# Attention on one core: the first batch's last K chunk and three Q tiles are staged in the next batch's V room

## Chip, cores, metric

The kernel runs on 1 core of one Trainium2 chip. The metric is device time in microseconds (us) of one execution; a profile also gives the span, some 2 us shorter. A run is taken as fast unless it is over 1.5% above the fastest of the same kernel. "PE" is the matrix engine, "DVE" the vector engine, "ACT" the scalar engine, "POOL" the engine that issues all converting loads, "SP" the one that issues stores and DMA transposes.

## The reference

Eight independent batches of softmax attention, sequence 2048, width 512, 32-bit:

```python
scores = np.matmul(q, k.transpose(0, 2, 1)) / np.sqrt(d_k)
attn_weights = special.softmax(scores, axis=-1)
return np.matmul(attn_weights, v)          # q, k, v: (8, 2048, 512)
```

## The kernel before

K, Q and V come in loads of 128 x 4 x 512 (1 MB read as 32-bit, 512 KB written as 16-bit), four to a batch and tensor. K and Q go to one of four staging buffers and are transposed from there, in the first batch by PE (except Q tiles 2 and 3), later by DMA. V goes straight to its own room, of which there are two, one for each of two neighbouring batches. The matmuls are in a Strassen-like form (seven products of half blocks in place of eight), so DVE makes sums of K, Q, V and P blocks beside them ("background"). A group `g` is one Q tile of 512 rows: four to a batch, 32 in all.

```python
stage = ctx.enter_context(tc.tile_pool(name="stage", bufs=4))
vpool = ctx.enter_context(tc.tile_pool(name="vpool", bufs=2))
# ... cut
def load(what, b, c, pieces=(CH,)):
    t = staged.get((what, b, c))
    if t is None:
        t = staged[what, b, c] = stage.tile([P, CH, D], F16, tag="stage", name="stage")
    n = CH - sum(pieces)
    for w in pieces:
        at = c * CH + n
        nc.gpsimd.dma_start(out=t[:, n:n + w, :], in_=srcs[what][b, :, at:at + w, :])
        n += w
# ... cut
def new_v(b):                       # V room: two memsets on POOL set its column of ones
    vh = vpool.tile([P, NJ, 2, VP], F16, tag="vh")
    t1 = vpool.tile([P, NJ, TP], F16, tag="t1")
    # ... cut
    nc.gpsimd.memset(vh[:, :, 1, D:D + 1], 1.0)
    nc.gpsimd.memset(t1[:, :, H:H + 1], 1.0)
# ... cut: what is fetched when, as (tile of the batch, slot)
    (0, 0, "newv"), (0, 2, "load", "v", 0), (0, 8, "load", "v", 1), # ... cut
    (1, 16, "load", "k", 0), (1, 26, "trans", "k", 0), (2, 8, "sum", "k", 0),
    (2, 8, "load", "k", 2), # ... cut
# ... cut: batch 1's loads are held back by a copy that needs P of group 1
            if what[0] == "newv":
                if g == 1:
                    nc.gpsimd.tensor_copy(out=gate[:], in_=pts[g][0][0][:, NJ - 1, 0:1])
                new_v(bb)
# ... cut: the start. k0 and q0 come through SP, in blocks
gate = const.tile([P, 1], F32)
nc.gpsimd.tensor_copy(out=gate[:], in_=firsts["q", 1][:, 0:1])
load("k", 0, 1, (2, 2))
load("k", 0, 2)
new_v(0)
load_v(0, 0)
# ... cut: transposes of k0, q0, k1 and the first score blocks on PE
load("k", 0, 3)
load("q", 0, 1)
for c in range(1, NCH):
    load_v(0, c)
for kb in range(2 * G, NKB):
    plain_tile(0, kb)
    # ... cut: PE transposes of k1, k2, k3, q1; DVE sums
load("q", 0, 2)
load("q", 0, 3)
```

The softmax here doesn't subtract the row's maximum and nothing guards it: scores larger than these inputs give would overflow.

## Time and profile before

| | before |
|---|---|
| time, median of 3 runs | 808.3 us (807.66 to 808.34) |
| span of the profiled run | 807.0 us |
| PE busy | 797.8 us, 99% |
| PE's waits in the first 60 us / after | 5.4 us / none |
| PE's wait for K chunk 3 | 1.36 us, from 20.93 to 22.29 |
| first product with V | 33.60 us |

PE sets the time; everything else matters only where it makes PE wait. The lines behind this table stand in the prediction below. In the profile's lines `stage` is a staging buffer, `vh` the V room, `raw` a transposed K or Q tile, `ks` and `qs` the sums made of such tiles, `cz` a piece of the scores that DVE adds up, `tr` and `t` PE's output banks.

### The profile page before, as it was taken

The page shows a single profiled execution, that of the slowest core. Times are in us where ns is not written, and L with a number is a line of the kernel's source. Part 1 is how long each engine was busy: PE and PEld are TensorE (multiplying, and loading weights), DVE is VectorE, ACT ScalarE, POOL GpSimd, SP SyncE. Part 2 cuts the span into 40 slices and gives each one's busy share as a digit, 9 for nine tenths or more (in the row PEclk, how much of TensorE's full clock was granted, in tenths as well). Part 3 has the DMA queues.
Part 4 walks back from the last instruction along what each step waited for, and adds up shares of the span by engine and source line. Part 5 has one row for each costly group of instructions (what it writes and reads, how often), then busy time and mean ns, then how long its engine had stood idle before and what let it go on. Part 6 is the DMA issues. An engine that isn't in the chain of part 4 may idle for free.

```text
span 807.0 us, 18446 instructions
## 1 busy us (share of the span) xinstructions
PE 797.8 (99%) x7244; PEld 704.6 (87%) x7244; DVE 591.0 (73%) x1477; ACT 570.2 (71%) x1039; POOL 72.5 (9%) x117
## 2 busy tenths in 40 slices
PE   8999999999999999999999999999999999999998
PEld 4688888888888888888888888888888888888887
DVE  4877787787767778677777777777777777766653
ACT  5767767677677677677677677777777776776773
POOL 4020103000030000300003000020002001000000
PEclk9999999999999999999999999999999999999999
DMA  9949995989379893898929997299972999921112
GB/s 206 198 91 190 211 166 106 205 161 171 92 130 213 154 168 82 145 208 153 164 79 148 219 151 149 69 177 191 162 164 62 190 200 154 155 71 48 54 40 79
DMA packets 190246, 116.56 MB, mean 144 GB/s; under 512 B 124496, under 2 KB 172880, under 8 KB 190160
## 3 DMA queue, kind: packets, MB, share of 16 engines
q0 software_dynamic: 49648, 49.29, 39.9%
q1 hardware_dynamic: 140368, 66.08, 39.5%
q8 instruction: 56, 0.92, 0.5%
q14 instruction: 30, 0.25, 0.1%
q10 hardware_dynamic: 144, 0.03, 0.0%
HBM read 100.70 MB, written 33.55 MB: 166 GB/s over the span
## 4 chain that ended last, share of the span: by engine, by line
PE 93%; DMA 4%; DVE 2%; ACT 0%; issue 0%; SPq 0%; DVEq 0%; ACTq 0%
PE t L378 47%; PE t L295 45%; DMA out_dram<-o 2%; DMA stage<-in_k_dram 1%; DMA cz<-in_q_dram 1%; PE t L233 0%; DVE cz L321 0%; PE tr L143 0%; DVE o L389 0%; SPq L115 0%; DVE raw L146 0%; DVE s L338 0%; DVE t L213 0%; DVE right L340 0%; DVE vh L211 0%
## 5 line engine op out<-in xcount | busy, mean ns | idle before, releaser
L295 PEld LDWEIGHTS <-raw 128*128 128x128 f16 x1984 | 194.1, 98 | 23.4 <-issue 0.6
L386 ACT ACTIVATE o<-t,r 128x256 f32<-128x256 f32 x256 | 122.2, 477 | 129.5 <-DVE r L406 104.0
L295 PE MATMUL t<-raw 128*128 128x256 f16 x1488 | 203.0, 273 | 0.0
L223 ACT ACTIVATE left<-t 128x512 f16<-128x512 f32 (+1 forms) x264 | 156.4, 594 | 21.8 <-PE t L295 19.3
L378 PEld LDWEIGHTS <-s 128*128 128x128 f16 x1536 | 150.3, 98 | 18.7 <-issue 0.4
L295 PEld LDWEIGHTS <-ks 128*128 128x128 f16 x1488 | 145.6, 98 | 18.2 <-issue 1.2
L389 DVE SCALAR_TENSOR_TENSOR o<-t,r,o 128x256 f32<-128x256 f32 x192 | 92.3, 481 | 81.2 <-PE t L378 48.6
L295 PE MATMUL t<-qs,ks 128*128 128x256 f16 x992 | 139.0, 273 | 0.5 <-ACT t L308 0.4
L223 ACT ACTIVATE right<-cz 128x1024 f16<-128x1024 f32 x124 | 132.5, 1068 | 1.5 <-DVE cz L318 1.5
L378 PE MATMUL t<-t,s 128*128 128x257 f16 (+1 forms) x1024 | 133.0, 273 | 0.0
L378 PE MATMUL t<-vh,left 128*128 128x256 f16 x1024 | 132.7, 273 | 0.0
L312 ACT COPY cz<-t 128x512 f32<-128x512 f32 x124 | 72.7, 586 | 67.3 <-PE t L295 67.3
L378 PEld LDWEIGHTS <-right 128*128 128x128 f16 x1024 | 100.2, 98 | 12.2 <-issue 0.6
L318 DVE TENSOR_TENSOR cz<-t,cz 128x512 f32<-128x512 f32 x124 | 85.1, 686 | 34.6 <-PE t L295 34.6
L378 PEld LDWEIGHTS <-left 128*128 128x128 f16 x1024 | 100.2, 98 | 11.6
L321 DVE TENSOR_TENSOR cz<-t,cz 128x512 f32<-128x512 f32 x124 | 84.7, 683 | 2.1 <-PE t L295 2.1
L295 PE MATMUL t<-qs,raw 128*128 128x256 f16 x496 | 74.4, 273 | 0.5 <-DVE cz L318 0.5
L295 PE MATMUL t<-raw,ks 128*128 128x256 f16 x496 | 74.4, 273 | 0.0
L338 DVE TENSOR_TENSOR s<-right 128x512 f16<-128x512 f16 x128 | 53.9, 421 | 27.5 <-ACT right L223 22.8
L315 ACT COPY cz<-t 128x512 f32<-128x512 f32 x124 | 73.1, 590 | 0.2 <-PE t L295 0.2
L308 ACT COPY t<-t 128x512 f32<-128x512 f32 x124 | 70.7, 570 | 3.3 <-ACT o L386 0.3
L378 PE MATMUL t<-vh,s 128*128 128x257 f16 x512 | 66.7, 273 | 0.1
(47 smaller groups left out, 611.6 us busy)
## 6 DMA issues: line engine op xcount, KB each, us to landing
out_dram<-o SPq DMA_DIRECT2D x127, 256.0 KB, 2.9
vh<-in_v_dram POOLq DMA_DIRECT2D x32, 512.0 KB, 13.8
stage<-in_q_dram POOLq DMA_DIRECT2D x31, 512.0 KB, 12.5
stage<-in_k_dram POOLq DMA_DIRECT2D x30, 512.0 KB, 8.5
raw<-stage SPq DMA_TRANSPOSE x58, 6.8
first<-in_q_dram SPq DMA_DIRECT2D x2, 256.0 KB, 3.7
first<-in_k_dram SPq DMA_DIRECT2D x2, 256.0 KB, 4.1
cz<-in_q_dram SPq DMA_DIRECT2D x2, 256.0 KB, 5.4
```

Of the source, the lines that this page charges most:

```text
L223: nc.scalar.activation(out=out_, in_=in_, func=EXP, scale=inv_sqrt_d)
L295: nc.tensor.matmul(dst[:, j * QH:(j + 1) * QH], lhs[:, j, c, :], rhs[:, :, c, :], start=(n in (1, 5) and j == 0 and c == 0), stop=(c == 1) ...
L308: nc.scalar.copy(out=self.y[:], in_=self.x[:])
L312: nc.scalar.copy(out=self.cz[:, :, 1, :], in_=self.two(self.z))
L315: nc.scalar.copy(out=self.cz[:, :, 0, :], in_=self.two(self.x))
L318: nc.vector.tensor_add(self.cz[:, :, 1, :], self.two(self.x), self.cz[:, :, 1, :])
L321: nc.vector.tensor_add(self.cz[:, :, 0, :], self.two(self.z), self.cz[:, :, 0, :])
L338: lambda: add(s1[:, js], a21, a22),
L378: nc.tensor.matmul(dst[:, 0:width], lhs(j), rhs(j), start=(first and j == 0), stop=(j == NJ - 1), skip_group_check=True,)
L386: nc.scalar.activation(out=out_, in_=src, func=COPY, scale=r[:])
L389: nc.vector.scalar_tensor_tensor(out=out_, in0=src, scalar=r[:], in1=out_, op0=MULT, op1=ADD)
```

## The change

The intent: in the first batch, four of the loads wait for a staging buffer to come free, and PE waits for one of them, K chunk 3. Batch 1's V room is empty then. K chunk 3 and Q tiles 1 to 3 are staged there, so that POOL issues all loads in one row, K chunk 3 and Q tile 1 ahead of V.

```diff
-    def load(what, b, c, pieces=(CH,)):
+    def load(what, b, c, pieces=(CH,), room=None):
         t = staged.get((what, b, c))
+        if room is not None:
+            t = staged[what, b, c] = room
         if t is None:
@@
+    spare = vpool.tile([P, NJ, 2, VP], F16, tag="vh", name="vh")
+    spare = spare[:].rearrange("p j s d -> p (j s d)")[:, 0:4 * CH * D]
+    spare = spare.rearrange("p (t n d) -> p t n d", t=4, n=CH)
     load("k", 0, 1, (2, 2))
     load("k", 0, 2)
+    load("k", 0, 3, room=spare[:, 0])
+    load("q", 0, 1, room=spare[:, 1])
     new_v(0)
-    load_v(0, 0)
+    for c in range(NCH):
+        load_v(0, c)
+    load("q", 0, 2, room=spare[:, 2])
+    load("q", 0, 3, room=spare[:, 3])
@@
-    load("k", 0, 3)
-    load("q", 0, 1)
-    for c in range(1, NCH):
-        load_v(0, c)
@@
-    load("q", 0, 2)
-    load("q", 0, 3)
```

## The prediction

> **What bounds the kernel now.** I read the page's busy shares first, then what the matrix engine waits for, then its instructions in order of time around the waits, then the POOL row of load issues with their landing times.
>
> ```profile
> PE 797.8 (99%) x7244; PEld 704.6 (87%) x7244; DVE 591.0 (73%) x1477; ACT 570.2 (71%) x1039; POOL 72.5 (9%) x117
> PE 93%; DMA 4%; DVE 2%; ACT 0%; issue 0%; SPq 0%; DVEq 0%; ACTq 0%
> ```
>
> The first line is busy time of each engine, the second the chain that ended last. The kernel is a stream of matmuls: 797.8 of the 807.0 us of span. Whatever touches only transfers can earn no more than PE's idle time, 807.0 - 797.8 = 9.2 us, less the 3.4 us after PE's last matmul (802.56 + 1.04 = 803.60). All of PE's waits, with the releaser (total us, times, longest):
>
> ```profile
> PE tr L143 <- DMA stage<-in_k_dram: 1.4, 1, 1.4
> PE t L537 <- DVE warm L510: 1.2, 1, 1.2
> PE tr L143 <- DVE stage L119: 0.9, 1, 0.9
> PE tr L143 <- ACT stage L119: 0.7, 1, 0.7
> PE t L295 <- DVE cz L318: 0.5, 1, 0.5
> PE t L295 <- ACT t L308: 0.4, 1, 0.4
> PE tr L143 <- DVE raw L146: 0.3, 1, 0.3
> ```
>
> That is 5.4 us, all in the first 60 us; the same view from 60 us on is empty. One line, the first, is a wait for one of the loads that the change moves. The others lie at the very start (warm, first tiles rounded to 16 bit) or are waits for DVE and ACT. PE in order of time, start and us, with the idle time before it in brackets:
>
> ```profile
> 17.31 3.62 PE L233 MATMUL t<-raw 128*128 128x512 f16 x16
> 22.29 1.07 PE L143 MATMUL tr<-ident,stage 128*128 128x128 f16 x16 [1.35 <-DMA stage<-in_k_dram]
> 23.19 2.75 PE L233 MATMUL t<-raw 128*128 128x512 f16 x12
> ```
>
> PE stops at 17.31 + 3.62 = 20.93 and starts the transposes of K chunk 3 (the program's last K chunk) at 22.29. The gap is 1.36 us, and the load it waits for is read from POOL's row:
>
> ```profile
> 6.60 2.29 POOL L105 DMA_DIRECT2D stage<-in_k_dram  x3
> 8.95 0.77 POOL L202 DMA_DIRECT2D vh<-in_v_dram  x1
> 10.22 0.75 POOL L105 DMA_DIRECT2D stage<-in_k_dram  x1 [0.51 <-DVE raw L146]
> 12.35 0.74 POOL L105 DMA_DIRECT2D stage<-in_q_dram  x1 [1.38 <-ACT right L223]
> 13.08 2.23 POOL L202 DMA_DIRECT2D vh<-in_v_dram  x3
> 15.95 0.74 POOL L105 DMA_DIRECT2D stage<-in_q_dram  x1 [0.64 <-PE tr L143]
> 17.77 0.74 POOL L105 DMA_DIRECT2D stage<-in_q_dram  x1 [1.08 <-PE tr L143]
> ```
>
> The third line is K chunk 3: issued 10.22 and, by the chain of waits, 12.02 us to landing, so there at 22.24. The brackets are waits for a staging buffer to come free, the waits that the change removes. Landing times (issue plus time to landing, each issue taken alone in the list of DMA issues; v2 and v3 from medians of two): k2 8.13+8.2 = 16.3; v0 8.95+10.9 = 19.85; k3 22.24; q1 12.35+12.5 = 24.85; v1 13.08+14.3 = 27.4; v2 29.9; v3 32.5; q2 15.95+19.0 = 34.95; q3 17.77+20.2 = 38.0. From k3 to q2 they land one every 2.55 us (12.7 us for five), whatever the spacing of their issues (0.74 to 2.1 us). The queue is therefore limited by transfer, not by issue: what counts is a load's place in the row, not its issue time.
>
> **What the Trainium skill says.** "DMA: Bandwidth & Descriptors", section Bandwidth, measures 425 GB/s for a large load and puts the ceiling at 435. A load here reads 1 MB of 32-bit data (128 x 4 x 512 x 4 B = 1.05 MB; the profile counts the 512 KB written), so 2.55 us each is 411 GB/s: the trace agrees that the row runs near its limit. The same page, section Queues, rings and completion order, says that each DMA engine takes descriptors in ring order; the landings in issue order agree. "SBUF — State Buffer", section SBUF: two separate sides, warns that certain DVE copies lock POOL out of writing descriptors; here POOL issues take 0.72 to 0.81 us with DVE copies beside them, so I give that little weight.
>
> **The change, part by part.** No engine but POOL changes its order: the compiled PE, DVE, ACT and SP streams hold the same operations in the same order, only the semaphore that a few wait on differs. POOL issues the same loads in the order k1 (two halves), k2, k3, q1, v0, v1, v2, v3, q2, q3.
>
> Removed: four buffer waits on POOL, 0.51 + 1.38 + 0.64 + 1.08 = 3.6 us of an engine that is 9% busy; not on the path. The row is not quite free: loads share eight completion semaphores, so v3 still waits for the first half of k1 to land (11.4), q2 for the second half (13.3), q3 for k2 (16.3). All three are early against a queue that is full to 35 us.
>
> Moved: k3 and q1 advance one place each, v0 falls back two. Giving each place its old landing time: k3 19.85 instead of 22.24, q1 22.24 instead of 24.85, v0 24.85 instead of 19.85; v1 to q3 keep theirs, because the bytes ahead of them are the same. (k3 could also gain a little because the row has no holes; I count none.)
>
> On the path: PE reaches k3's transposes at 20.93, and k3 is there at 19.85 with 1.08 us to spare. The 1.36 us gap goes. q1's transposes would start at 25.78 - 1.36 = 24.42, with q1 there since 22.24. Next, from 26.43 to 33.1, DVE is the bound (its chain starts at the copy that follows q1's transposes: "26.43 0.69 DVE raw L146"), and again from 41.9 to 49.0. Both start from PE's transposes, so they move as a block; DVE's order is fixed, so the gain neither grows nor shrinks there. From 60 us PE has no wait, and batch 1's loads hang on a gate on POOL that follows ACT (53.13), so they move along with the rest. Sum: 808.3 - 1.36 = 806.9 us.
>
> **Rivals.**
> 1. The wait moves to V. The first product with V starts at 33.60 and its fourth pair of matmuls, which needs v3, at about 33.60 + 6 x 0.109 = 34.25; moved up, 32.9, against v3's landing at 32.5. Only 0.4 us to spare: v3 landing a microsecond late gives back 0.6, time 807.5. For it: v3's place is unchanged while its user advances. Against: same bytes ahead.
> 2. k3 does not land on v0's old time. From 11 to 14 us the queue moved only 113 to 145 GB/s (as counted), against 206 later, and I do not know why; if more waiting loads lengthen that stretch, k3 lands after 20.93 and every microsecond beyond is lost. At k3 = 21.5 the time is 807.5; at 22.2, 808.2.
> 3. The gain is swallowed. q2's and q3's DMA transposes keep their absolute times (35.02 + 4.9 = 39.9; 38.1 + 4.8 = 42.9), but DVE first uses q2 at 47.15 - 1.36 = 45.8, 6 us later. Batch 1's V, whose room now holds k3 and the Q tiles, must wait for those transposes at 42.9, but its gate opens near 51.8. Neither bites: no loss.
> 4. More than the gap is won. DVE idles 2.50 us before k3's copy (22.94), which suggests up to 2.5; but 1.15 of it is PE's own transpose and copy latency, which stays. Time 805.8 only if it all counted.
>
> **Range and chances.** Full gain about 65%, partial (rivals 1 and 2) 25%, none or slightly worse 10%. Three runs of before spread over 0.7 us, so the median of after may stray half a microsecond by itself. Range 805.9 to 808.2. A change of over 2% is 16 us, and PE's whole waiting is 5.4, so faster by 2% is as good as excluded; slower by 2% would need a wait repeated in every batch, and later batches keep their order and waits.
>
> **What would show it.** Right: PE's list of waits without the K line and 1.4 us shorter in sum; PE busy through 21 to 22 us; k3 landing near 19.9, q1 near 22.2, v0 near 24.9, v3 still near 32.5; POOL's eleven loads without buffer waits, the last issued just after 16.3; DVE's block starting at 25.1 and the first product with V at 32.2. Wrong: a wait of PE for a V load near 33, k3 landing after 20.9, or a new wait after 60 us.

## The result, and the profile after

| | before | after |
|---|---|---|
| time, median of 4 runs | 808.32 us | 808.55 us (807.29 to 809.25) |
| ratio | | 0.9999, 95% interval 0.9982 to 1.0017 |
| span of the profiled run | 807.0 us | 807.4 us |
| first product with V | 33.60 us | 32.66 us |
| PE's waits after 60 us | none | 1.4 us |

A ratio is the mean time of one kernel's fast runs over that of the other's fast runs of the same rounds, so it is not quite the ratio of the medians quoted. The time did not change. All waits of PE in the changed kernel, with the releaser (us in total, times, longest; lines are numbered 2 to 11 higher than before):

```profile
PE t L548 <- DVE warm L512: 1.2, 1, 1.2
PE t L297 <- DVE cz L320: 0.9, 3, 0.5
PE t L297 <- DVE cz L323: 0.9, 1, 0.9
PE tr L145 <- DMA stage<-in_k_dram: 0.7, 2, 0.4
PE t L297 <- ACT t L310: 0.4, 1, 0.4
PE tr L145 <- DVE raw L148: 0.3, 1, 0.3
```

The list sums to 4.4 us, 1.0 less than before, but sums of waits do not compare the two starts: the 0.9 + 0.7 us for the first tiles (`stage L119`) are missing here, and PE ran its matmuls near 5 us slower instead (0.63 us for four transposes, not 0.39; the trace's first record of a fully granted clock is at 7.1 us, not 4.6). The 1.4 us for K chunk 3 are gone (the 0.7 us of `stage<-in_k_dram` are waits for the earlier chunks 1 and 2), but there is a new line, `cz L323`. First the part that was meant, PE in order of time (start, us, then the idle time before in brackets):

```profile
12.95 0.62 PE L145 MATMUL tr<-ident,stage 128*128 128x128 f16 x8 [0.41 <-DMA stage<-in_k_dram]
...
17.00 1.07 PE L145 MATMUL tr<-ident,stage 128*128 128x128 f16 x16 [0.30 <-DMA stage<-in_k_dram]
17.90 3.62 PE L235 MATMUL t<-raw 128*128 128x512 f16 x16
21.36 1.06 PE L145 MATMUL tr<-ident,vh 128*128 128x128 f16 x16
```

The transposes of K chunk 3 (they now read `vh`) start with no gap. POOL's row, in order of time:

```profile
6.62 2.43 POOL L107 DMA_DIRECT2D stage<-in_k_dram  x3
9.04 0.75 POOL L107 DMA_DIRECT2D vh<-in_k_dram  x1
...
13.18 0.74 POOL L204 DMA_DIRECT2D vh<-in_v_dram  x1 [0.34 <-DMA stage<-in_k_dram]
...
17.23 0.74 POOL L107 DMA_DIRECT2D vh<-in_q_dram  x1 [2.04 <-DMA stage<-in_k_dram]
```

No buffer waits are left, only those on the eight completion semaphores. K chunk 3 landed at 19.47, Q tile 1 at 21.98, V 0 at 24.52, V 3 at 32.16. At the first product with V PE is 0.94 us ahead of the kernel before, and stays so to 87 us. Then, near 91, PE in order of time:

```profile
91.59 1.03 PE L297 MATMUL t<-qs,ks 128*128 128x256 f16 x8 [0.89 <-DVE cz L323]
...
93.71 0.60 PE L297 MATMUL t<-qs,raw 128*128 128x256 f16 x4 [0.21 <-DVE cz L320]
```

The chain of waits leads back from there to one transfer (start, us, what):

```profile
73.41 15.50 DMA raw<-stage
...
88.92 0.44 DVE ks L175
...
90.86 0.68 DVE cz L323
```

It is the DMA transpose of batch 1's K chunk 0. DVE stands 3.2 us at the sum of that chunk (`ks L175`), and the additions PE needs (`cz`) come behind it on the same engine. The sum in DVE's order of time, before and after:

```profile
86.59 0.41 DVE L173 TENSOR_TENSOR ks<-raw 128x512 f16<-128x512 f16 x1
88.92 0.42 DVE L175 TENSOR_TENSOR ks<-raw 128x512 f16<-128x512 f16 x1 [3.18 <-DMA raw<-stage]
```

In the kernel before the same transpose was issued at 74.34 and took 10.2 us; it was there at 84.5, two us ahead of its sum at 86.59. In the changed kernel it took 15.5. The Trainium skill, "TensorE: Matmul & The Clock Gate", section Architectural detail, says that DVE's queue is strictly first in, first out; the trace agrees, as the `cz` additions did not pass the waiting sum. Both traces have all 7244 matmuls, so matmuls can be compared by their number: between the 700th and the 900th the changed kernel falls back by 1.42 us against the kernel before. This is where the gain went.

Why is that transpose late? Batch 1's row of loads is held back by the gate. POOL at that point, before:

```profile
53.13 0.18 POOL L486 CAST gate<-left 128x1 f32<-128x1 f16 x1 [34.62 <-ACT left L223]
53.25 0.13 POOL L195 MEMSET vh<- 128x8 f16 x1
...
53.73 0.75 POOL L105 DMA_DIRECT2D stage<-in_q_dram  x1 [0.30 <-PE t L295]
```

and after:

```profile
52.20 0.18 POOL L488 CAST gate<-left 128x1 f32<-128x1 f16 x1 [34.23 <-ACT left L225]
52.49 0.13 POOL L197 MEMSET vh<- 128x8 f16 x1
...
52.97 0.75 POOL L107 DMA_DIRECT2D stage<-in_q_dram  x1 [0.30 <-issue]
```

From gate to memset it is 0.12 us before and 0.29 after: the memset writes to the room in which K and Q were staged, and in the compiled order it now carries waits on seven semaphores instead of two, all long reached (the last transpose out of the room had landed at 42.26). The packed trace has the wait instructions: one ahead of the memset before (53.19), three after (52.21, 52.29, 52.38), 0.09 us apart; two more of them make the 0.17 us. It is not the other room: e_v_swap below trades the rooms and has 0.12 us. So the row starts 0.77 us after the gate instead of 0.60. SP's third output store does not move with it: it is issued 0.50 us after the row's first load before, 0.33 us after. In the trace's packets, the row's first one now comes 2.15 us after its issue instead of 1.46, behind the store's instead of ahead of them, and the row runs slower: its first load takes 8.0 us instead of 6.4, its seventh 26.4 instead of 23.1. What follows in this document tests that chain.

### The profile page after: what moved, and what is told of

It reads as the page before. It is cut to its first block, busy times and chain, and to the rows that moved or that the text cites. A ratio compares the mean times of both kernels' runs of the same rounds, so it can differ in the third digit from the quotient of the medians.

```text
span 807.4 us, 18443 instructions
## 1 busy us (share of the span) xinstructions
PE 799.1 (99%) x7244; PEld 705.4 (87%) x7244; DVE 590.3 (73%) x1477; ACT 570.4 (71%) x1039; POOL 72.8 (9%) x117
## 4 chain that ended last, share of the span: by engine, by line
PE 90%; DMA 6%; DVE 3%; issue 0%; ACT 0%; POOL 0%; SPq 0%; DVEq 0%; ACTq 0%
PE t L380 46%; PE t L297 44%; DMA raw<-stage 4%; DMA stage<-in_k_dram 1%; PE t L235 1%; DMA first<-in_q_dram 1%; PE tr L145 0%; DVE o L391 0%; DVE cz L323 0%; DVE cz L320 0%; DVE s L340 0%; POOL stage L107 0%; DVE s L343 0%; ACT o L388 0%; DVE right L342 0%
## 5 line engine op out<-in xcount | busy, mean ns | idle before, releaser
L320 DVE TENSOR_TENSOR cz<-t,cz 128x512 f32<-128x512 f32 x124 | 85.1, 686 | 34.5 <-PE t L297 34.5
L323 DVE TENSOR_TENSOR cz<-t,cz 128x512 f32<-128x512 f32 x124 | 84.7, 683 | 1.9 <-PE t L297 1.9
## 6 DMA issues: line engine op xcount, KB each, us to landing
stage<-in_q_dram POOLq DMA_DIRECT2D x28, 512.0 KB, 10.4
```

Source lines behind the costliest of these rows:

```text
L320: nc.vector.tensor_add(self.cz[:, :, 1, :], self.two(self.x), self.cz[:, :, 1, :])
L323: nc.vector.tensor_add(self.cz[:, :, 0, :], self.two(self.z), self.cz[:, :, 0, :])
```

## The experiments

Twelve runs, in four calls; all gave correct results. Those of one call ran on the same chip beside the same runs of the kernel before; for e_k2_gate, alone in the last call, eleven of the twelve runs of the kernel before are those of the second call.

### before_again: the unchanged kernel against itself

No edit.

> The unchanged kernel against itself, for the size of the noise. In the first profile PE waited 1.36 us for K chunk 3 and not at all after 60 us. Theory A (the later wait in the changed kernel, 1.4 us of PE waiting at 91 to 94 us, comes with the change): here again no PE wait after 60 us, the batch-1 K transposes issued near 74 land within 11 us. Theory B (that wait is a matter of chance in the transfers of batch 1): it may show here too. Ratio 1.000 in any case; k1's first half lands near 11.4, k2 near 16.3 if the first profile was typical.

Ratio 0.9997 (0.9985 to 1.001). PE waited 1.6 us for K chunk 3 and had no wait after 60 us; batch 1's transpose took 10.4 us. Theory A stands. The run also shows the noise: its five times go from 807.0 to 808.9.

### after_again: the changed kernel again

No edit to the changed kernel.

> The changed kernel again. Theory A: PE again waits 1 to 1.5 us for DVE near 91 us and the ratio stays at 1.000. Theory B: the wait at 91 us is absent or of another size. Both: no PE wait for K chunk 3. Theory D (deep row: more loads in the queue slow the earlier ones): k1's first half lands again at 12.5 to 13 and k2 near 16.9, and PE waits for both, 0.4 and 0.3 us. Rival to D (chance): k1 near 11.4 and k2 near 16.3 as before, then ratio 0.9983 (minus 1.36 us).

Ratio 0.9999 (0.9985 to 1.0013). PE waited again, 0.5 us for `cz L323` and 0.2 for `cz L320`, near 90 us; the transpose took 15.1 us. The sum, 0.7 us, is below the 1 to 1.5 us expected of theory A, and theory B had allowed for another size, so this run alone does not decide. Theory B falls by all runs together: the wait and a transpose of 15.1 to 15.8 us are in all four profiles with this start of the row (after, after_again, e_gate_v, after_third), and in none of before, before_again, e_order_only and e_v_swap. But there was no wait for K chunks 1 and 2 this time: chunk 1's first half landed at 10.63, chunk 2 at 14.52. So theory D, that a deep row slows the first loads, is not supported: the start of the kernel varies from run to run.

### e_order_only: the order alone

Edit to the kernel before:

```diff
     load("k", 0, 2)
-    new_v(0)
-    load_v(0, 0)
@@
     load("k", 0, 3)
     load("q", 0, 1)
-    for c in range(1, NCH):
+    new_v(0)
+    for c in range(NCH):
         load_v(0, c)
```

> The kernel before with only the first V load moved behind K chunk 3 and Q tile 1; all buffer waits stay, nothing is staged in the V room. If the place in the row is what counts, k3 lands near v0's old 19.9 or earlier, the 1.36 us wait of PE goes, and because the row is no deeper than before k1 lands near 11.4 and k2 near 16.3: PE reaches the first product with V 1.36 us earlier, at about 32.2. Time 806.9 if nothing later gives it back. If instead the issue time counted, k3 (still issued near 10.2) would land near 22 and the wait would stay.

806.72 us, ratio 0.998 (0.9967 to 0.9992). POOL in order of time still shows a buffer wait at K chunk 3:

```profile
9.95 0.74 POOL L105 DMA_DIRECT2D stage<-in_k_dram  x1 [0.78 <-DVE raw L146]
```

K chunk 3 landed at 19.97 although it was issued about as late as before (9.95 against 10.22 and 9.49): the place in the row counts, not the time of issue. PE's wait for it is gone (0.5 us for K chunk 2 is left), and there is no wait after 60 us, with batch 1's transpose at 10.1 us. The whole gain of the change comes from moving V 0 behind two other loads; the staging in the V room is not needed for it.

### e_gate_v: the changed kernel with V held back

```diff
     load("q", 0, 1, room=spare[:, 1])
+    nc.gpsimd.tensor_copy(out=gate[:], in_=staged["k", 0, 1][:, CH - 1, 0:1])
     new_v(0)
```

> The changed kernel with one small POOL copy ahead of V that waits for the second half of k1, so that only five loads stand in the row until about 13.3 us. Theory D: k1's first half back near 11.4, k2 near 16.3, no PE wait for either, first product with V at about 32.2, 0.4 to 0.7 us better at that point than the changed kernel. Rival to D (chance, or POOL's back-to-back issuing): k1 and k2 as late as in the changed kernel, or early in both.

807.9 us, ratio 0.9991 (0.9979 to 1.0004). Chunk 1's first half landed at 10.98, chunk 2 at 16.15, the first product with V began at 31.87. That is within what the changed kernel itself did in its two profiles (10.63 and 12.90; 14.52 and 16.95), so the run does not speak for theory D. Near 91 us PE waited as in the changed kernel, 1.2 + 0.2 us, with a transpose of 15.8 us.

### e_row_first: the changed kernel, batch 1's first load ahead of the memsets

```diff
+        if g == 1 and slot == 0:
+            nc.gpsimd.tensor_copy(out=gate[:], in_=pts[g][0][0][:, NJ - 1, 0:1])
+            todo = todo[::-1]
         for what in todo:
@@
             if what[0] == "newv":
-                if g == 1:
-                    nc.gpsimd.tensor_copy(out=gate[:], in_=pts[g][0][0][:, NJ - 1, 0:1])
                 new_v(bb)
```

> The changed kernel with one swap on POOL in batch 1: the first Q load of the row is issued right after the gate, ahead of the two memsets that prepare V's room (the memset there waits for six semaphores). In the traces so far the row's first load comes 0.50 to 0.54 us before the third output store in the kernels without staging in the V room and 0.33 us before it in those with it, the store's packets then go first, and batch 1's row runs slower: its last V load takes 26.1 to 26.4 us instead of 23.1 to 23.3, K chunk 0's DMA transpose 15.1 to 15.8 instead of 10.1 to 10.4, and PE waits 0.7 to 1.4 us for DVE near 91. Theory O (the order of row and store decides): here the last V load takes about 23 us, the transpose about 10, no PE wait after 60 us, and the ratio falls to 0.998 or below. Theory R (the room V goes to decides: buffer 0 instead of 1): row still slow, PE wait still there, ratio near 0.9995.

806.79 us, ratio 0.9984 (0.9971 to 0.9996). POOL in order of time:

```profile
51.48 0.18 POOL L479 CAST gate<-left 128x1 f32<-128x1 f16 x1 [35.16 <-ACT left L225]
52.02 0.75 POOL L107 DMA_DIRECT2D stage<-in_q_dram  x1 [0.35 <-PE t L297]
52.76 0.15 POOL L197 MEMSET vh<- 128x8 f16 x1
```

The row starts 0.54 us after the gate, the store follows 0.55 us later, the row's first load takes 6.45 us, its seventh 23.4, the transpose 10.4, and PE's list of waits after 60 us is empty. One instruction moved ahead of two small memsets brings the gain back. Theory O holds against theory R; e_row_later below limits it. (The memset of the changed kernel waits for seven semaphores, not six as expected above.)

### e_v_swap: the kernel before with the two V rooms exchanged

```diff
+    vpool.tile([P, NJ, 2, VP], F16, tag="vh", name="vh")
     new_v(0)
```

> The kernel before with one unused V tile allotted first, so that V of batch 0 and 1 trade rooms; nothing else moves. Theory R: batch 1's row slow (last V load 26 us, transpose 15 us), a PE wait of 0.5 to 1.4 us near 92, ratio 1.001 to 1.002. Theory O: row as before (23 us, 10 us), no PE wait after 60 us, ratio 1.000. Both: the 1.4 to 1.6 us wait for K chunk 3 stays.

808.62 us, ratio 1.0005 (0.9992 to 1.0018). Seventh load 23.4 us, transpose 11.5 us, no PE wait after 60 us. Theory R fell: it is not the room. (The profiled execution, 810.8 us, had slow first loads, chunk 1's first half at 13.88; the other five took 807.0 to 808.7.)

### e_row_late: the kernel before with the row held back a little

```diff
                 if g == 1:
-                    nc.gpsimd.tensor_copy(out=gate[:], in_=pts[g][0][0][:, NJ - 1, 0:1])
+                    for n in range(3):
+                        nc.gpsimd.tensor_copy(out=gate[:], in_=pts[g][0][0][:, NJ - 1, n:n + 1])
```

> The kernel before with the gate copy of batch 1 made three times, so that its row of loads starts 0.2 to 0.4 us later and behind the store. Theory O: the row turns slow (last V load 26 us, transpose of K chunk 0 15 us) and PE waits 0.5 to 1.4 us for DVE near 92 us; time up by about that, ratio 1.001 to 1.002. Theory R: nothing changes beyond 0.3 us, no PE wait after 60 us.

The store now comes 0.09 us after the row's first issue. The row starts 1.01 us after the gate instead of 0.60. It is slower, though less than in the changed kernel (seventh load 24.3 us), and the transpose takes 14.7 us. PE waits 0.2 us near 94 us, less than the 0.5 to 1.4 expected. DVE's waits between 80 and 92 us begin with:

```profile
DVE ks L173 <- DMA raw<-stage: 2.4, 1, 2.4
```

Between the 700th and the 900th matmul PE falls back 0.65 us. So a delay of some 0.4 us on POOL makes the same late transpose in the otherwise unchanged kernel. The time, 808.42 us, ratio 1.0008 (0.9996 to 1.0021), leans the same way but does not leave the noise.

### e_v_first: three places later

```diff
     new_v(0)
-    load_v(0, 0)
+    for c in range(NCH):
+        load_v(0, c)
@@
     load("q", 0, 1)
-    for c in range(1, NCH):
-        load_v(0, c)
```

> The kernel before with all four V loads ahead of K chunk 3: the dose test of the place theory. K chunk 3 falls back three places of 2.5 us and should land near 29.8 instead of 22.2, PE's wait for it should grow from 1.4 to about 9 us, and the time rise by about 7.6 us to 816 (ratio 1.0094). If issue time or total depth counted rather than place, it would rise by less than 3 us.

818.19 us, ratio 1.0126 (1.0113 to 1.0139): 9.8 us, more than expected. K chunk 3 landed at 29.55, the 7.3 us later that three places foretell. The rest is seen in PE's order of time:

```profile
29.60 1.89 PE L143 MATMUL tr<-ident,stage 128*128 128x128 f16 x16 [8.65 <-DMA stage<-in_k_dram]
31.28 4.15 PE L233 MATMUL t<-raw 128*128 128x512 f16 x12
```

The same two groups took 1.07 and 2.75 us in the kernel before. After 8.65 us of idling PE ran slower for a while, which adds 0.8 + 1.4 = 2.2 us, a cost missing from my expectation; 7.3 + 2.2 = 9.5. The Trainium skill, "TensorE: Matmul & The Clock Gate", section Part 1: The HAM clock gate, has PE fall to half rate when it idles; the trace agrees, with a granted clock of 0.50 from 24 to 34 us.

### e_row_later: the row held back until the store is over

As e_row_late, with `range(12)`.

> The kernel before with twelve gate copies instead of one, so that batch 1's row of loads starts some 2 us later and the third output store (2.5 us alone) is over before the first packet of the row. If the slow row needs the store's packets in flight just ahead of its own, the row is fast again: from the issue of its first load to the landing of its seventh 27.5 to 27.9 us, as in the kernel before, not 30.5 to 30.8. If it is enough that the store is issued first, it stays near 30. Whichever holds, K chunk 0 comes 2 us later than before, its transpose may then be late by itself, so a PE wait near 92 us of up to 1 us and a ratio of 1.000 to 1.002 are possible in both cases.

The row's first load came 2.14 us after the store's issue. Its first packet came 1.46 us after issue again, and its first two loads took 5.6 and 8.4 us: as fast as before (6.4 and 8.2) and not as in the changed kernel (8.0 and 10.5). So it seems that the slow beginning needs the store's packets just ahead of the row's (one profile). But from the third load on it was slow, seventh 25.2 us, probably because SP's next stores and Q's transpose, which do not move with POOL, now meet an earlier part of the row; the measure that I had named, issue to seventh landing, was 29.6 us, nearer the other branch. The transpose took 16.0 us and PE waited 1.4 + 0.2 us. 809.59 us, ratio 1.002 (1.0006 to 1.0034): starting the row late costs time by itself.

### e_row_first_again and after_third: side by side

No new edits.

> The changed kernel with the row's first load ahead of the memsets, a second time and beside the changed kernel on the same chip: row of 27.5 to 27.9 us, transpose of K chunk 0 near 10.4 us, no PE wait after 60 us, ratio 0.998 (0.997 to 0.9995). If the first result was chance, the PE wait near 91 us is back.

806.63 us, ratio 0.9978 (0.9965 to 0.9992); seventh load 23.5 us, transpose 10.5, no PE wait after 60 us.

> The changed kernel a third time: the store 0.33 us after the row's first issue, row 30.5 to 30.8 us, transpose above 15 us, PE wait of 0.7 to 1.4 us in sum between 88 and 95 us, ratio 0.9990 to 1.0005, and PE some 1 us behind the variant of the same job at the end.

807.56 us, ratio 0.9998 (0.9985 to 1.0011); the store 0.33 us after the row's issue, seventh load 25.2 us (the row, at 29.6 us, is a little better than I had expected), transpose 15.1, PE waits of 0.5 + 0.2 us near 90. Between the 700th and the 900th matmul the changed kernel falls back by 1.02 us against the kernel before, the variant by nothing.

### e_k2_gate: the changed kernel, batch 1's K chunk 2 held back

```diff
             elif what[0] == "load":
+                if g == 2 and what[1:] == ["k", 2]:
+                    nc.gpsimd.tensor_copy(out=gate[:], in_=kT[1, 0][0][:, 0, 0, 0:1])
```

> The changed kernel with one POOL copy ahead of batch 1's load of K chunk 2, so that this load waits until K chunk 0's DMA transpose has landed; the start of the row is left slow (store 0.33 us after the row's first issue, first two loads 7.9 to 8.0 and 10.3 to 10.5 us). In the traces the load of K chunk 2 is issued near 80.7 to 82.2 when Q's transpose lands, and where V's last load is late its packets run beside the transpose of K chunk 0. Link held by my theory: the transpose is late because it shares the engines with that load. Then here it takes about 11 us or a little more (not 15), PE's 0.5 to 0.9 us wait for cz L323 near 90 is gone, and the ratio falls to 0.998 to 0.999. Rival: the transpose is late because the row ahead of it ends late; then it still takes 14 to 15 us and the wait stays.

The row was left slow (first load 8.0 us, seventh 26.2), and the transpose took 12.45 us instead of 15.1 to 15.5; the wait near 90 us is gone. So about half of the 5 us by which the transpose is late comes from sharing the engines with the load of K chunk 2. That the rest comes from the late end of the row ahead of it, the rival, fits but is not tested by itself. The Trainium skill, "DMA: Bandwidth & Descriptors", section Queues, rings and completion order, says that each engine goes round robin between the queues it has work for; a transpose that slows when a load on the other queue is there, and speeds up when it is kept away, agrees with that. But POOL then issues K chunks 2 and 3 together, late:

```profile
85.73 1.50 POOL L107 DMA_DIRECT2D stage<-in_k_dram  x2
```

and PE, in order of time, pays further on, as the transpose of K chunk 1 takes 17.5 us:

```profile
106.20 0.39 PE L380 MATMUL t<-t,s 128*128 128x257 f16 x2 [0.73 <-DVE s L340]
```

From the 700th to the 1000th matmul PE falls back 1.29 us against the kernel before, all after the 850th. 807.32 us, ratio 1.0001 (0.9972 to 1.0029): inconclusive as a time, with one run at 814.0 at a clock of 0.995. It was run at another time. It serves for the link alone.

## Why the prediction was wrong

**What bounds, and the removed wait: right.** PE's 1.36 us wait for K chunk 3 is absent in all three profiles of the changed kernel. K chunk 3 landed at 19.47, 17.58 and 17.73 (foretold 19.85), V 3 at 32.16, 30.47 and 31.51 (foretold 32.5).

**"A load's place in the row" counts, not its issue time: right.** e_order_only gained without any earlier issue, and in e_v_first three places cost K chunk 3 7.3 us. One reading in the prediction says too much: its 411 GB/s counts bytes read, while half as many were written (206 GB/s), so a row at the skill's ceiling is not shown; that loads land every 2.55 us whatever the spacing of their issues is.

**The size of the early gain: in agreement, but not measured closely.** The first product with V began at 33.60, 33.48, 35.28, 33.49 and 32.59 us in the five profiles whose first batch is that of the kernel before, mean 33.7, and at 32.66, 31.49, 31.69, 31.93, 31.75 and 31.90 in the six of the changed kernel, e_row_first and e_k2_gate, mean 31.9. The difference is 1.8 us; without e_v_swap, whose first loads were slow, 1.4; and 0.8 when it is also counted from the issue of the row's first load, which came at 5.1 to 6.6 us. The foretold 1.36 lies among them; single executions differ by more than a microsecond, because the first loads of the kernel land at different times (chunk 1's first half at 10.2 to 13.9 us).

**The step that failed: "From 60 us PE has no wait, and batch 1's loads hang on a gate on POOL that follows ACT (53.13), so they move along with the rest", and rival 3's "Neither bites: no loss".** I had asked whether batch 1's V room would be free in time, and it was, by some 10 us. I had not asked what else a start of batch 1's row hangs on. The prediction says that "only the semaphore that a few wait on differs", and did not ask what that costs. The row did not move along with the rest: the waits on the memset, though all reached, put 0.17 us between the gate and the row; the store of SP then went ahead of the row's packets; the row ran 2 to 3 us slower; the DMA transpose of K chunk 0 took 15.1 to 15.5 us instead of 10.2 to 10.4; DVE stood at that chunk's sum with the additions PE needs behind it; and PE fell back 1.42, 1.01 and 1.02 us in the three profiles. e_row_first and e_row_first_again show the row's start to be the cause: they take away only this, and the ratio goes to 0.9984 and 0.9978. e_row_late makes the same late transpose in the kernel before; e_v_swap excludes the room; e_k2_gate shows the link from the transpose to PE's wait near 90 us.

**The margin that I did not look at** was in the profile before: that transpose landed at 84.5 and its sum ran at 86.59, so there were two microseconds to spare, at a transfer whose duration (4.8 us at 38 us with little else in the queues, 10.2 at 74, 19.7 at 62) depends on what else is in the queues.

**What stays open.** Why the row runs slower for some 8 us when the store's packets go just ahead of it is not shown. Nor is the order of store and row the whole of it: in e_row_later the store was over, the first two loads were fast, and the row was slow all the same from the third on (seventh 25.2 us), so a late start of the row has a cost of its own. And the sum closes only roughly: 1.4 us gained (1.8 with e_v_swap) and 1.0 to 1.4 given back leave 0 to 0.4 (0.4 to 0.8), while the three ratios, 0.9999, 0.9999 and 0.9998, say 0.1 to 0.2. Their intervals are over 1 us wide on each side, so nothing here asks for a further cause.

**A better version.** e_row_first (806.79 and 806.63 us) and e_order_only (806.72) beat the kernel before by 1.3 to 1.8 us, 0.16 to 0.22%, with intervals that leave out 1. The changed kernel is 0.9 us (after_third against e_row_first_again) and 1.6 us (after_again against e_order_only) slower by the medians; no interval was worked out for that. e_order_only is the simpler one.

## What to carry to other kernels

When one wait is removed from a kernel that is otherwise full, follow what is borrowed to its next owner: a buffer lent out comes back with waits on its first writer, and even waits that are long reached can move a queue's start by a fraction of a microsecond (0.17 us here). Look through the chain for transfers that end shortly before an engine needs them in a fixed order, and ask how their duration changes when two queues trade places. In a row of loads limited by transfer, change the order first: it cost no buffer here and gave all there was to gain.

## What the Trainium skill lacked or had wrong

- "DMA: Bandwidth & Descriptors" has no figure for a DMA transpose beside other traffic. The same 512 KB transpose of a staged chunk took 4.8 us with little else in the queues, 10.2 us near 74 us, 15.1 to 15.8 in the changed kernel, 19.7 beside a full row of loads.
- No page has the effect of order between a store and a row of loads: with the store's packets just ahead, as in the changed kernel, the row's first load took 8.0 us instead of 6.4 and its seventh 25.2 to 26.4 instead of 23.1 to 23.5.
- No page gives a cost for waits on semaphores already reached (the nearest is a figure for reading a semaphore's value); from gate to memset on POOL it was 0.12 us with two semaphores to wait for and 0.29 us with seven.
